# A decoder trunk whose weight blocks are stored as even columns then odd columns, and read in turn

## The chip, the cores and the metric

The kernel runs on one core of one Trainium2 chip. The metric is the device time of one execution in microseconds (us); lower is better. All the weights, some 410 MB, are read from device memory once in each execution. The weights are laid out by the host before the launch, and that is not timed.

## The reference, cut to what matters

Two layers on 256 tokens of width 2048. Each has a mixer (a recurrent block in the first, dilated attention in the second) and an MLP with a squared ReLU, each behind an RMSNorm, and the trunk ends with one more RMSNorm. Everything is float32.

```python
def _mlp(h, w1, w2):                                   # w1 2048 x 8192, w2 8192 x 2048
    u = jnp.einsum('bsd,df->bsf', h, w1)
    u = jnp.square(jax.nn.relu(u))
    return jnp.einsum('bsf,fd->bsd', u, w2)

def _rglru_block(h, w_in, conv_w, conv_b, w_a, b_a, w_x, b_x, lam, w_out):
    xg = jnp.einsum('bsd,de->bse', h, w_in)            # 2048 x 5120
    ...
    return jnp.einsum('bse,ed->bsd', y, w_out)         # 2560 x 2048

def _dilated_attention_block(h, w_qkv, w_o):
    qkv = jnp.einsum('bsd,de->bse', h, w_qkv).reshape(bsz, s, 3, N_HEADS, HEAD_DIM)
    ...
    return jnp.einsum('bse,ed->bsd', o.reshape(bsz, s, D_MODEL), w_o)

def reference(x, ...):
    for i in range(DEPTH):                             # DEPTH = 2
        h = _rmsnorm(x, mix_norm[i])
        ...
        x = x + _rglru_block(...) if i % 2 == 0 else x + _dilated_attention_block(...)
        x = x + _mlp(_rmsnorm(x, mlp_norm[i]), mlp_w1[i], mlp_w2[i])
    return _rmsnorm(x, final_norm)
```

## The kernel before

**Split operands.** A float32 operand is cut in two: a high part that the copy into the type float32r makes (ScalarE, line 132) and a low part, the difference (VectorE, line 136). A product of matrices is then three TensorE products: high by high, high by low, low by high. All of them are issued by one helper, `mm` (line 201), so that nearly every TensorE row of the profile has that line; the names of the tiles tell them apart. `whi` and `wlo` are the parts of a block of weights; `xT`, `aT` and `sT` are parts of tokens, 128 wide at a time.

**Weights.** They come in blocks of 128 partitions by 2048 float32 (1 MB, `UW`), one transfer each, into the tile `raw` (or `q...` in the MLP). A block holds four pieces of 512 columns in a row, one for each of four steps over the contracted dimension.

**Two kinds of products.** A matmul on TensorE has a stationary operand, 128 by 128, which is loaded first (LDWEIGHTS), and a moving operand that is streamed past it, up to 512 columns.

- In `stand_w` the weights are stationary and the tokens move, 256 columns at a time. The profile names such products `g<-xT,whi` or `acc<-xT,whi`: the first name behind the arrow is the moving operand. They serve w_in, the q and k part of w_qkv, and w1.
- In `stand_x` and in the `product` of the MLP's groups the tokens are stationary and the weights move, 512 columns at a time. The profile names them `acc<-whi,aT`, `tr<-whi,sT` and so on, with the weights first. They serve w_out, the v part of w_qkv, w_o and w2. Each step calls `three` (line 310) for its three products; where `border` is set the last one is cut into two of 256 columns. The last rows of the last chunk have their own loop, `last_half`, in pieces of 256 columns.

**The second MLP matrix** is worked in groups of two by two blocks with seven products in place of eight; sums of weight blocks are made by VectorE (line 649) and by accumulating transfers from GpSimd's queue (line 645), sums of tokens by VectorE. These sums are made element by element on whole blocks.

**Order.** A list of items, one for each block of weights, is written out by the planners (`plan_rec`, `plan_mlp`, `plan_att`). Ahead of each item the loads of blocks five ahead and the splits of blocks two or three ahead are issued; behind it, what its result feeds. Nothing reorders the list, and each engine works it off in turn.

**Layouts.** `_layout` permutes the weights on the host. `move` gives the blocks of w_out, w_v and w_o, and a line of its own gives w2: (block, partition, step, column), the 512 columns of a piece one behind another.

The stages in the order of the profile: recurrent input products to about 250 us, w_out to 370, first MLP to 1010, v, q, k and attention to 1345, w_o to 1430, second MLP to the end.

## Time and profile before

| what | value |
|---|---|
| median of 3 executions | 2086.66 us (2085.65 to 2086.71) |
| span of the profiled execution, first to last instruction | 2083.2 us |
| median less span: what lies around the instructions | 3.5 us |
| TensorE matmuls busy | 2071.8 us (99%) |
| VectorE / ScalarE / GpSimd busy | 82% / 61% / 4% |
| read from device memory | 409.58 MB, 198 GB/s over the span |
| mean granted TensorE clock | 0.999 |

The profile gives no other time for the profiled execution than its span, so 2083.2 + 3.5 us stands for it. A matmul's own duration (277 ns for 256 columns, 390 ns for 512) holds the time from its first column to its last result; matmuls overlap, so the pace is read from the spacing of their starts or from the length of a long unbroken piece of one kind, not from the mean duration. The column "busy" counts overlapping time once.

### The profile page before, as it was taken

The page shows a single profiled execution, that of the slowest core. Times are in us where ns is not written, and L with a number is a line of the kernel's source. Part 1 is how long each engine was busy: PE and PEld are TensorE (multiplying, and loading weights), DVE is VectorE, ACT ScalarE, POOL GpSimd, SP SyncE. Part 2 cuts the span into 40 slices and gives each one's busy share as a digit, 9 for nine tenths or more (in the row PEclk, how much of TensorE's full clock was granted, in tenths as well). Part 3 has the DMA queues.
Part 4 walks back from the last instruction along what each step waited for, and adds up shares of the span by engine and source line. Part 5 has one row for each costly group of instructions (what it writes and reads, how often), then busy time and mean ns, then how long its engine had stood idle before and what let it go on. Part 6 is the DMA issues. An engine that isn't in the chain of part 4 may idle for free.

```text
span 2083.2 us, 33880 instructions
## 1 busy us (share of the span) xinstructions
PE 2071.8 (99%) x14231; PEld 1905.6 (91%) x14231; DVE 1713.7 (82%) x1927; ACT 1278.7 (61%) x1388; POOL 86.7 (4%) x83
## 2 busy tenths in 40 slices
PE   9999999999999999999999999999999999999998
PEld 8999988999999999899889999889999998998996
DVE  7988855799999989998558868756999999899985
ACT  7777865566566656665546556555666566566553
POOL 0111100000000000000000000000000000000001
PEclk9999999999999999999999999999999999999999
DMA  8555555677887788777554455456778877887773
GB/s 300 204 204 193 200 202 182 236 230 243 298 245 255 251 261 268 222 259 228 204 182 173 171 182 180 171 183 235 242 243 285 248 258 244 266 276 218 251 240 141
DMA packets 68920, 472.59 MB, mean 227 GB/s; under 512 B 7584, under 2 KB 7712, under 8 KB 13472
## 3 DMA queue, kind: packets, MB, share of 16 engines
q1 hardware_dynamic: 60560, 411.45, 53.4%
q0 software_dynamic: 8064, 58.72, 14.4%
q8 instruction: 111, 1.82, 0.3%
q14 instruction: 41, 0.34, 0.0%
q10 hardware_dynamic: 144, 0.26, 0.0%
HBM read 409.58 MB, written 2.10 MB: 198 GB/s over the span
## 4 chain that ended last, share of the span: by engine, by line
PE 98%; DMA 1%; DVE 0%; ACT 0%; SPq 0%; issue 0%; ACTq 0%
PE acc L201 46%; PE g L201 32%; PE tr L201 19%; PE tr L242 1%; DMA raw<-in_w_in 0%; DMA xg<-in_xT 0%; PE tr L816 0%; DVE wlo L136 0%; ACT whi L132 0%; ACT xT L1039 0%; SPq L1025 0%; ACT junk L904 0%; PE tr L276 0%; SPq L1023 0%; DVE xc L902 0%
## 5 line engine op out<-in xcount | busy, mean ns | idle before, releaser
L132 ACT ACTIVATE whi<-raw 128x2048 fp32r<-128x2048 f32 (+1 forms) x309 | 569.7, 1846 | 403.8 <-PE acc L201 195.9
L136 DVE TENSOR_TENSOR wlo<-raw,whi 128x2048 fp32r<-128x2048 f32 (+1 forms) x309 | 678.0, 2197 | 108.0 <-ACT whi L132 107.5
L201 PE MATMUL g<-xT,whi 128*128 128x256 f32 x3649 | 626.6, 277 | 0.0
L201 PEld LDWEIGHTS g<-xT,whi 128*128 128x128 f32 x3649 | 550.0, 188 | 0.0
L201 PE MATMUL g<-xT,wlo 128*128 128x256 f32 x1824 | 503.9, 276 | 0.1
L201 PE MATMUL acc<-xT,whi 128*128 128x256 f32 x2724 | 466.5, 277 | 0.4 <-ACT whi L132 0.3
L201 PEld LDWEIGHTS acc<-xT,whi 128*128 128x128 f32 x2724 | 410.8, 188 | 1.7 <-ACT whi L132 1.2
L201 PE MATMUL acc<-xT,wlo 128*128 128x256 f32 x1360 | 376.0, 276 | 0.0
L201 PEld LDWEIGHTS g<-xT,wlo 128*128 128x128 f32 x1824 | 342.6, 188 | 0.2 <-DVE wlo L136 0.2
L201 PE MATMUL acc<-whi,aT 128*128 128x512 f32 (+1 forms) x1064 | 334.1, 389 | 0.0
L132 ACT ACTIVATE whi<-q 128x2048 fp32r<-128x2048 f32 x112 | 215.1, 1921 | 130.0 <-PE g L201 94.6
L136 DVE TENSOR_TENSOR wlo<-q,whi 128x2048 fp32r<-128x2048 f32 x112 | 256.1, 2286 | 30.6 <-ACT whi L132 30.6
L201 PEld LDWEIGHTS acc<-xT,wlo 128*128 128x128 f32 x1360 | 255.4, 188 | 0.5 <-DVE wlo L136 0.4
L201 PEld LDWEIGHTS acc<-whi,aT 128*128 128x128 f32 x1064 | 199.3, 188 | 40.2
L201 PE MATMUL tr<-whi,sT 128*128 128x512 f32 (+1 forms) x728 | 221.0, 376 | 0.0
L201 PE MATMUL acc<-wlo,aT 128*128 128x512 f32 (+1 forms) x532 | 206.4, 388 | 0.0
L132 ACT ACTIVATE whi<-qT 128x2048 fp32r<-128x2048 f32 x56 | 107.6, 1921 | 125.6 <-PE g L201 92.8
L201 PEld LDWEIGHTS tr<-whi,sT 128*128 128x128 f32 x728 | 136.6, 188 | 34.1 <-issue 7.0
L201 PE MATMUL tr<-whi,aT 128*128 128x512 f32 (+1 forms) x462 | 145.2, 383 | 0.0
L136 DVE TENSOR_TENSOR wlo<-qT,whi 128x2048 fp32r<-128x2048 f32 x56 | 128.1, 2287 | 11.9 <-ACT whi L132 11.9
L201 PE MATMUL tr<-wlo,sT 128*128 128x512 f32 x336 | 131.0, 390 | 0.0
L201 PEld LDWEIGHTS acc<-wlo,aT 128*128 128x128 f32 x532 | 100.0, 188 | 19.7
(169 smaller groups left out, 2127.1 us busy)
## 6 DMA issues: line engine op xcount, KB each, us to landing
raw<-in_w SPq DMA_DIRECT2D x172, 1024.0 KB, 6.3
q<-in_w SPq DMA_DIRECT2D x84, 1024.0 KB, 7.2
raw<-in_w_in SPq DMA_DIRECT2D x35, 1024.0 KB, 4.9
raw<-in_w_qk SPq DMA_DIRECT2D x32, 1024.0 KB, 4.8
q<-q POOLq DMA_DIRECT2D x28, 1024.0 KB, 12.5
q<-qT POOLq DMA_DIRECT2D x28, 1024.0 KB, 7.0
raw<-in_w_out SPq DMA_DIRECT2D x20, 1024.0 KB, 4.8
raw<-in_w_v SPq DMA_DIRECT2D x16, 1024.0 KB, 4.8
```

The lines of the kernel that those rows point to most:

```text
L132: nc.scalar.activation(split[i][0][:, s], r, AF.Copy)
L136: nc.vector.tensor_sub(split[i][1][:, s], r, split[i][0][:, s].bitcast(F32))
L201: nc.tensor.matmul(o, l, r, start=start, stop=stop, skip_group_check=True)
L242: nc.tensor.transpose(tr[:, k, t * 128:(t + 1) * 128], xc[n][:, t, c:c + 128], ident)
```

## The change

The columns of every 512-column piece of the moving weights (w_out, w_v, w_o, w2) are stored in another order: the 256 even columns first, then the 256 odd ones. The products that move these weights read them through a view with two dimensions, 256 steps outside and 2 inside: element 0 of the first half, element 0 of the second half, element 1 of the first half, and so on. In a partition's memory two columns that follow each other in the stream lie 256 elements (1024 bytes) apart, and the next step goes back by 255 elements. The columns reach the array in their old order, so the output, its layout and every later step stay as they were. Where a product covers 256 of the 512 columns, it reads 128 of each half.

No instruction is added, removed or moved on any engine or queue, and no tile or transfer has another size: the list of instructions is the same but for the line numbers and the access pattern of the moving operand. Blocks in `stand_w`, the gate weights and the token tiles stay as they were.

```diff
     def three(bank, xh, xl, hi, lo, opens, closes, border):
 
-        mm(bank, xh, hi, opens, False)
-        mm(bank, xh, lo, False, False)
+        mm(bank, xh, in_turn(hi), opens, False)
+        mm(bank, xh, in_turn(lo), False, False)
         cut = 256 if border else 512
         for at in range(0, 512, cut):
-            mm(bank[:, at:at + cut], xl, hi[:, at:at + cut], False, closes and at + cut == 512)
+            mm(bank[:, at:at + cut], xl, in_turn(hi, at, cut), False, closes and at + cut == 512)
+
+    def in_turn(w, at=0, n=512):
+
+        return w.rearrange("p (t q) -> p q t", t=2)[:, at // 2:(at + n) // 2, :]
...
             for s in halves:
                 for j, k in enumerate(rows[1]):
                     xh, xl = aT(k)[:, 128:256], aT(k)[:, 384:512]
-                    w = slice(j * 512 + s.start, j * 512 + s.stop)
-                    mm(acc[1][:, s], xh, hi[:, w], False, False)
-                    mm(acc[1][:, s], xh, lo[:, w], False, False)
-                    mm(acc[1][:, s], xl, hi[:, w], False, j == 3)
+                    wh, wl = (in_turn(w[:, j * 512:(j + 1) * 512], s.start, 256) for w in (hi, lo))
+                    mm(acc[1][:, s], xh, wh, False, False)
+                    mm(acc[1][:, s], xh, wl, False, False)
+                    mm(acc[1][:, s], xl, wh, False, j == 3)
...
     def move(w):
         k, n = w.shape
-        return c(w.reshape(k // 512, 4, 128, n // 512, 512).transpose(3, 0, 2, 1, 4)).reshape(-1, 128, UW)
+        w = w.reshape(k // 512, 4, 128, n // 512, 256, 2).transpose(3, 0, 2, 1, 5, 4)
+        return c(w).reshape(-1, 128, UW)
...
-        w2 = mlp_w2[i].reshape(4, 4, 4, 128, 4, 512).transpose(0, 4, 1, 3, 2, 5)
+        w2 = mlp_w2[i].reshape(4, 4, 4, 128, 4, 256, 2).transpose(0, 4, 1, 3, 2, 6, 5)
```

## Prediction

> **What bounds the kernel now.** I read the page first: its span, the busy shares, and the chain that ended last.

> ```profile
> span 2083.2 us, 33880 instructions
> PE 2071.8 (99%) x14231; PEld 1905.6 (91%) x14231; DVE 1713.7 (82%) x1927; ACT 1278.7 (61%) x1388; POOL 86.7 (4%) x83
> PE 98%; DMA 1%; DVE 0%; ACT 0%; SPq 0%; issue 0%; ACTq 0%
> ```

> TensorE is busy 99% of the span and makes 98% of the chain. Outside its work there are only 2083.2 - 2071.8 = 11.4 us, at the two ends. So whatever makes TensorE's stream longer makes the kernel longer by the same amount, and whatever makes it shorter counts until another engine becomes the bound. The next question is its pace, which busy time cannot tell since matmuls overlap. The chain in order of time has long pieces of one kind, and their length over their count is the spacing.

> ```profile
> 55.10 21.78 PE acc L201 x192
> 252.07 16.34 PE acc L201 x72
> ```

> The first piece (start, length, count) is 192 products of 256 moving columns in the recurrent stage: 21.78 / 192 = 0.1134 us each. The second is 72 products of 512 moving columns in w_out, the kind that the change touches: 16.34 / 72 = 0.2269 us. The second is twice the first, so there is nothing per instruction to see; both come to **0.443 ns per column**. The stream is paced by columns.

> **What the change touches.** It adds, removes and moves no instruction. The transfers and the splits keep their sizes and their contiguous patterns, and the sums of blocks work element by element, so the new order in a block is nothing to them: they cost what they cost, and if one of these took longer, TensorE's work would cover it as it does now. The one thing that is new is the order of addresses in the moving operand. How many products that is stands in the groups of TensorE by line and shape:

> ```profile
> L201 PE MATMUL acc<-whi,aT 128*128 128x512 f32 x1048 | 331.3, 390 | 0.0
> L201 PE MATMUL acc<-wlo,aT 128*128 128x512 f32 x524 | 204.1, 390 | 0.0
> L201 PE MATMUL tr<-whi,sT 128*128 128x512 f32 x616 | 198.9, 393 | 0.0
> L201 PE MATMUL tr<-whi,aT 128*128 128x512 f32 x434 | 139.6, 390 | 0.0
> L201 PE MATMUL tr<-wlo,sT 128*128 128x512 f32 x336 | 131.0, 390 | 0.0
> L201 PE MATMUL tr<-wlo,aT 128*128 128x512 f32 x224 | 87.4, 390 | 0.0
> L201 PE MATMUL acc<-whi,xT 128*128 128x512 f32 x254 | 79.8, 392 | 0.0
> L201 PE MATMUL acc<-whi,sT 128*128 128x512 f32 x212 | 68.9, 389 | 0.0
> L201 PE MATMUL acc<-wlo,xT 128*128 128x512 f32 x128 | 50.1, 391 | 0.0
> L201 PE MATMUL acc<-wlo,sT 128*128 128x512 f32 x112 | 43.6, 389 | 0.0
> ...
> L201 PE MATMUL tr<-whi,sT 128*128 128x256 f32 x112 | 22.2, 280 | 0.0
> ...
> L201 PE MATMUL tr<-whi,aT 128*128 128x256 f32 x28 | 5.5, 280 | 0.0
> ...
> L201 PE MATMUL acc<-whi,sT 128*128 128x256 f32 x24 | 4.8, 280 | 0.0
> ...
> L201 PE MATMUL acc<-whi,aT 128*128 128x256 f32 x16 | 3.0, 282 | 0.0
> L201 PE MATMUL acc<-wlo,aT 128*128 128x256 f32 x8 | 2.3, 283 | 0.0
> ...
> L201 PE MATMUL acc<-whi,xT 128*128 128x256 f32 x4 | 0.8, 280 | 0.0
> ```

> The ten rows of 512 columns add up to 3888, the six of 256 to 192, which is 96 more in units of 512: **3984 products of 512 columns**, 2.040 million columns. No record is missing: `whi` products are twice the `wlo` products in every pair (1048 + 8 to 524 + 4, 616 + 56 to 336, 434 + 14 to 224, 254 + 2 to 128, 212 + 12 to 112). At 0.2269 us they take 904 us now, 43% of the span, and each 0.01 ns per column is worth 20.4 us. The other products move tokens (`xT` ahead of the weight's name) and are not touched.

> **What a column costs when its neighbour is 1024 bytes away.** No row of this trace has it: every large stream here is read contiguously. It must be bounded.

> From below: a gain is possible, since the pace need not be the array's own. The trace has one slower stream to hold it against, ten bfloat16 products at the start.

> ```profile
> 1.25 4.45 PE L201 MATMUL g<-junk 128*128 128x512 bf16 x10 [1.25 <-DVE junk L1005]
> L201 PE MATMUL g<-junk 128*128 128x512 bf16 x10 | 4.4, 631 | 1.3 <-DVE junk L1005 1.3
> ```

> Ten products in 4.45 us, the last of which takes 0.63: nine spacings of 0.424 us. If that is the array at half its pace, which I suppose and the trace does not show, full pace is 0.212 us for 512 columns, an estimate, and the float32r stream at 0.2269 loses 7% to something, about one column time in 16. That loss grows with columns, so it belongs to reading them or to their type. This is the lower end: 0.0147 us less for each of 3984 products, -59 us.

> [...]

> From above: what does it cost an engine to fetch a float32 column by itself? The nearest rows are ScalarE and VectorE on the same weights, in two sizes.

> ```profile
> L132 ACT ACTIVATE whi<-raw 128x2048 fp32r<-128x2048 f32 x291 | 558.4, 1919 | 402.1 <-PE acc L201 195.9 <-PE g L201 84.9 <-PE tr L201 41.7
> L132 ACT ACTIVATE whi<-raw 128x512 fp32r<-128x512 f32 x16 | 9.3, 620 | 1.7 <-DMA raw<-in_w_first 1.7
> L136 DVE TENSOR_TENSOR wlo<-raw,whi 128x2048 fp32r<-128x2048 f32 x291 | 665.2, 2286 | 106.4 <-ACT whi L132 106.1
> L136 DVE TENSOR_TENSOR wlo<-raw,whi 128x512 fp32r<-128x512 f32 x16 | 10.5, 688 | 1.6 <-ACT whi L132 1.4
> ```

> ScalarE takes (1919 - 620) / 1536 = 0.846 ns for one more column, VectorE (2286 - 688) / 1536 = 1.040 ns. TensorE streams the same data at 0.443 ns, twice as fast as ScalarE. That is why I expect a loss: an engine that gets two columns in the time in which ScalarE gets one probably fetches neighbours together, and after the change no two columns that follow each other are neighbours. If each then needs a fetch of its own, the pace falls to that of one column at a time. I take ScalarE's **0.846 ns** for it. Exactly half of today's pace, 2 x 0.443 = 0.886, and the pace of the ten products, 0.424 / 512 = 0.829, lie on both sides of it; VectorE's 1.040 is the upper end.

> [...]

> **The sum.** (0.846 - 0.443) ns x 2.040 million columns = +822 us. Nothing hides it: TensorE has no idle time inside these stages. Then 2083.2 + 822 + 3.5 us of what lies around the span (median 2086.66 less 2083.2) gives **2908 us**. With 0.829 it is 2874, with 0.886 it is 2990, with 1.040 it is 3304. The other engines only wait longer.

> **Rivals.**

> *The pace stays.* If the addresses are made one by one and the memory answers each at full pace, the order is free and the time is 2087 us. For it: spacing is exactly proportional to columns in two kinds of streams from two kinds of tiles, as if the array set it. Against it: the 7% against the bfloat16 stream. [...]

> *The lost sixteenth goes.* If the 7% is a wait in reading one run of addresses (a place in memory that needs a pause before it answers again), two runs in turn give each place twice the time, and the wait is gone. Price: up to -59 us, 2028 us. It decides as soon as the pause is shorter than one column's time in the other half. VectorE would not stop it; in the first MLP it stands so:

> ```profile
> 410.00:1010.00 600.00, 600.00 (x4030) 548.31 (x4030) 541.48 (x511) 365.85 (x311) 24.20 (x28) 1.00 0.78 250
> ```

> Of 600 us TensorE has all and VectorE 541.5 (the columns are the stretch, then busy time of matmuls, weight loads, VectorE, ScalarE and GpSimd). The stretch holds less than a third of the 59 us to be gained, some 20 us, and VectorE's slack in it is 58.5 us. Against this rival: it needs a memory that likes jumps better than runs, and nothing here shows one.

> [...]

> *A small loss*, a pause at some steps only, lies anywhere between 2091 and 2870 us; I have no row for it.

> **How the numbers follow.** Forecast, one column at a time (2874 to 2990): 0.33. The pace of VectorE or worse: 0.11. A small loss: 0.09. Pace stays: 0.20. The sixteenth goes, wholly or in part: 0.27. So faster by over 0.2% (4 us, about what a measurement of this kernel can tell from no change) 0.27, within 0.2% 0.20, slower 0.53. The range must reach over both signs: from the lower end, 2028, to VectorE's pace, 3304. Only about a tenth lies outside, above it. The forecast's own range is 2874 to 2990.

> **What would show it.** In the changed profile the long piece of 72 products at the start of w_out should take 72 x 0.433 = 31.2 us in place of 16.34, and that of 192 at 55.10 should stay at 21.78; TensorE's share stays at 99% and VectorE's falls to some 59%. [...] If the piece of 192 changed too, or VectorE's rows grew, the cause would lie outside the moving reads and my reasoning would be wrong.

## The result, and the profile after

| | before | changed |
|---|---|---|
| median | 2086.26 us | 2052.54 us |
| all executions | 2085.65 to 2086.71 | 2049.91 to 2054.89 |
| ratio (95% interval) | | 0.9839 (0.9825 to 0.9853) |

The kernel before has one execution more here than in the table ahead of the change. One execution of a later kernel (w2 alone), in a slower state at 7365 us, is left out of all medians and ratios. The changed kernel is 1.6% faster, where I had forecast it 39% slower. The page of the changed kernel answers to the three lines that opened the prediction (span; busy time; the chain that ended last):

```profile
span 2049.2 us, 33880 instructions
PE 2031.2 (99%) x14231; PEld 1910.6 (93%) x14231; DVE 1712.1 (84%) x1927; ACT 1278.3 (62%) x1388; POOL 87.1 (4%) x83
PE 88%; DVE 5%; issue 3%; ACT 2%; DMA 1%; SPq 0%; ACTq 0%; DVEq 0%
```

TensorE's busy time fell by 40.6 us and the span by 34.0. TensorE made 98% of the chain before and makes 88% now: other engines have come into it, VectorE first. The pieces of the chain that the prediction named say what happened to the pace (start, length, count):

```profile
78.92 21.91 PE acc L201 x192
...
103.65 21.78 PE acc L201 x192
...
251.29 15.54 PE acc L201 x72
```

Products that move tokens stayed at 21.78 us for 192 (one piece has 0.13 us more). The 72 products that move w_out went from 16.34 to 15.54 us: **0.2158 us each in place of 0.2269**. The stream runs at 0.4215 ns per column, not at 0.846.

Over 3984 products that is 3984 x 0.0111 = 44 us. The median fell by 33.7. Most of the other 10 us is a wait, of which the list of TensorE's waits shows a part (in total, times, longest):

```profile
PE tr L201 <- DVE xc L657: 4.6, 14, 0.3
PE g L201 <- DVE junk L1009: 1.3, 1, 1.3
```

The list of the kernel before has no row like the first. But the list counts only time in which TensorE is idle, and a product's last results overlap a short wait: each lasts 0.38 us in the rows below, at a spacing of 0.216. By the starts of the products there are 28 such places: in 14 of them (the row's) the first product behind the wait starts 0.49 us later than the pace gives, in 14 others 0.23 us later, 10.1 us in all; in the kernel before the same places lose 1.2 us. The products right behind them lose 1.1 us more than before. One of the places of the second kind in order of time, TensorE and then VectorE, in the first MLP (start, length):

```profile
528.59 0.38 PE L201 MATMUL tr<-wlo,aT 128*128 128x512 f32 x1
528.80 0.38 PE L201 MATMUL tr<-whi,aT 128*128 128x512 f32 x1
529.25 0.45 PE L201 MATMUL tr<-whi,sT 128*128 128x512 f32 x1
```

```profile
525.88 2.29 DVE L136 TENSOR_TENSOR wlo<-qT,whi 128x2048 fp32r<-128x2048 f32 x1
528.09 0.42 DVE L572 TENSOR_TENSOR aT<-uu,aT 128x256 fp32r<-128x256 f32 x1
528.42 0.68 DVE L657 TENSOR_TENSOR xc<-xc,tr 128x512 f32<-128x512 f32 x1
```

The next group product needs a `tr` bank that VectorE is still emptying into `xc`. That take ends at 528.42 + 0.68 = 529.10, the product starts at 529.25, and the gap to the product before it is 0.45 us in place of 0.216. VectorE had no pause ahead of it: its three rows follow each other. In the kernel before the same place stood so:

```profile
537.12 0.39 PE L201 MATMUL tr<-whi,aT 128*128 128x512 f32 x1
537.35 0.43 PE L201 MATMUL tr<-whi,sT 128*128 128x512 f32 x1
536.48 0.68 DVE L653 TENSOR_TENSOR xc<-xc,tr 128x512 f32<-128x512 f32 x1
```

There the product kept its spacing of 0.23 us and started 0.19 us behind the end of the take (537.16); now it starts 0.15 us behind it. So this take had only some 0.04 us to spare before the change. The first question is why two places in turn are read faster than one run, and the second is whether VectorE's queue is what gives a quarter of the gain back.

### The profile page after: what moved, and what is told of

Read it like the earlier page. It is cut to its first block, busy times and chain, and to the rows that moved or that the text cites. A ratio compares the mean times of both kernels' runs of the same rounds, so it can differ in the third digit from the quotient of the medians.

```text
span 2049.2 us, 33880 instructions
## 1 busy us (share of the span) xinstructions
PE 2031.2 (99%) x14231; PEld 1910.6 (93%) x14231; DVE 1712.1 (84%) x1927; ACT 1278.3 (62%) x1388; POOL 87.1 (4%) x83
## 4 chain that ended last, share of the span: by engine, by line
PE 88%; DVE 5%; issue 3%; ACT 2%; DMA 1%; SPq 0%; ACTq 0%; DVEq 0%
PE acc L201 44%; PE g L201 31%; PE tr L201 13%; DVE wlo L136 2%; ACT whi L132 2%; DVE xc L657 1%; DVE qT L653 1%; DMA q<-in_w 0%; DVE aT L572 0%; PE tr L242 0%; DMA xg<-in_xT 0%; PE tr L820 0%; DVE uu L563 0%; ACT xg L244 0%; DVE xT L218 0%
## 5 line engine op out<-in xcount | busy, mean ns | idle before, releaser
L132 ACT ACTIVATE whi<-raw 128x2048 fp32r<-128x2048 f32 (+1 forms) x309 | 569.0, 1844 | 375.7 <-PE acc L201 201.8
L136 DVE TENSOR_TENSOR wlo<-raw,whi 128x2048 fp32r<-128x2048 f32 (+1 forms) x309 | 677.0, 2196 | 96.4 <-ACT whi L132 95.4
L201 PE MATMUL g<-xT,whi 128*128 128x256 f32 x3649 | 627.7, 277 | 0.0
L201 PEld LDWEIGHTS g<-xT,whi 128*128 128x128 f32 x3649 | 550.5, 188 | 0.0
L201 PE MATMUL g<-xT,wlo 128*128 128x256 f32 x1824 | 504.5, 277 | 0.0
L201 PE MATMUL acc<-xT,whi 128*128 128x256 f32 x2724 | 466.6, 277 | 0.2 <-ACT whi L132 0.2
L201 PEld LDWEIGHTS acc<-xT,whi 128*128 128x128 f32 x2724 | 410.9, 188 | 1.3 <-ACT whi L132 1.1
L201 PE MATMUL acc<-xT,wlo 128*128 128x256 f32 x1360 | 376.3, 277 | 0.4 <-DVE wlo L136 0.4
L201 PEld LDWEIGHTS g<-xT,wlo 128*128 128x128 f32 x1824 | 342.5, 188 | 0.4 <-DVE wlo L136 0.4
L201 PE MATMUL acc<-whi,aT 128*128 128x512 f32 (+1 forms) x1064 | 322.6, 378 | 0.0
L132 ACT ACTIVATE whi<-q 128x2048 fp32r<-128x2048 f32 x112 | 214.7, 1917 | 117.8 <-PE g L201 91.9
L136 DVE TENSOR_TENSOR wlo<-q,whi 128x2048 fp32r<-128x2048 f32 x112 | 256.1, 2287 | 26.9 <-ACT whi L132 26.4
L201 PEld LDWEIGHTS acc<-xT,wlo 128*128 128x128 f32 x1360 | 255.3, 188 | 0.9 <-DVE wlo L136 0.8
L201 PEld LDWEIGHTS acc<-whi,aT 128*128 128x128 f32 x1064 | 200.6, 189 | 27.4
L201 PE MATMUL tr<-whi,sT 128*128 128x512 f32 (+1 forms) x728 | 213.7, 366 | 5.5 <-DVE xc L657 4.6
L201 PE MATMUL acc<-wlo,aT 128*128 128x512 f32 (+1 forms) x532 | 200.8, 377 | 0.0
L132 ACT ACTIVATE whi<-qT 128x2048 fp32r<-128x2048 f32 x56 | 107.5, 1920 | 126.5 <-PE g L201 91.5
L201 PEld LDWEIGHTS tr<-whi,sT 128*128 128x128 f32 x728 | 137.4, 189 | 33.9 <-issue 16.0
L201 PE MATMUL tr<-whi,aT 128*128 128x512 f32 (+1 forms) x462 | 140.1, 373 | 0.0
L136 DVE TENSOR_TENSOR wlo<-qT,whi 128x2048 fp32r<-128x2048 f32 x56 | 128.1, 2287 | 7.2 <-ACT whi L132 5.6
L201 PE MATMUL tr<-wlo,sT 128*128 128x512 f32 x336 | 127.4, 379 | 0.0
L201 PEld LDWEIGHTS acc<-wlo,aT 128*128 128x128 f32 x532 | 100.6, 189 | 13.4
```

The lines of the kernel that those rows point to most:

```text
L132: nc.scalar.activation(split[i][0][:, s], r, AF.Copy)
L136: nc.vector.tensor_sub(split[i][1][:, s], r, split[i][0][:, s].bitcast(F32))
L201: nc.tensor.matmul(o, l, r, start=start, stop=stop, skip_group_check=True)
```

## The experiments

### The order by itself

A kernel of products alone: one stationary tile for each type, and for each order 40 products in a row, of 512 columns unless the row says less. In the code, `two(t, q)` cuts `t * q` columns into `t` runs of `q` and reads one column of each run in turn; in the other patterns, the order of the letters behind the arrow is the order of reading.

```diff
+    ("again", lambda w: w[:, 0:512]),
+    ("halves", two(2, 256)), ("quarter", two(4, 128)), ("sixteen", two(16, 32)), ("evenodd", two(256, 2)),
+    ("swapd", lambda w: w[:, 0:512].rearrange("p (b t q) -> p b q t", t=2, q=4)),
+    ("swapb", ... q=2), ("swaph", ... q=8), ("swapp", ... q=16), ("swapz", ... q=64),
+    ("runsb", lambda w: w[:, 0:512].rearrange("p (t q r) -> p q t r", t=2, r=2)), ("runsd", ... r=4),
+    ("stepb", lambda w: w[:, 0:1024].rearrange("p (q t) -> p q t", t=2)[:, :, 0]),
...
```

> A kernel of products alone, 40 in a row of each kind, all of 512 columns unless said, to measure the spacing by the order in which the moving operand is read; the trunk's computation is left out. Known from the changed kernel: columns one behind another 227 ns, two halves in turn 216 ns. Theory 'place': neighbours in memory read one behind another conflict in a small unit of memory; then every order whose next column lies in another unit gives 216 (quarters, sixteen parts, apart by 4 to 64 columns), while pairs swapped within four columns and runs of 16 or 64 columns keep 227. Theory 'form': a plain pattern of step 1 is read in a wide way that loses a sixteenth, any pattern whose innermost step is not 1 is read column by column at 216; then also pairs 2 columns apart, even columns before odd ones, and every second column of 1024 give 216, and any innermost run (2, 4, 16, 64 columns) gives 227. Theory 'distance': two far places are needed; then only halves, quarters and 64 apart give 216, and 2 to 16 apart give 227. The bfloat16 series: 216 in both orders if the loss belongs to the four-byte type. 256 token columns: 113 plain and 108 to 110 in turn. Output written in pairs of two places: 227 if the array's output does not mind, more if it does.

TensorE in order of time. A row is one series; the start of the next row less its own, over 40, is the spacing.

```profile
19.44 8.79 PE L73 MATMUL bank<-halves,st 128*128 128x512 f32 x40
28.07 9.25 PE L73 MATMUL bank<-again,st 128*128 128x512 f32 x40
37.16 11.46 PE L73 MATMUL bank<-quarter,st 128*128 128x512 f32 x40
48.45 17.57 PE L73 MATMUL bank<-sixteen,st 128*128 128x512 f32 x40
65.83 18.24 PE L73 MATMUL bank<-evenodd,st 128*128 128x512 f32 x40
83.89 8.82 PE L73 MATMUL bank<-swapd,st 128*128 128x512 f32 x40
92.54 9.24 PE L73 MATMUL bank<-swapb,st 128*128 128x512 f32 x40
101.62 8.80 PE L73 MATMUL bank<-swaph,st 128*128 128x512 f32 x40
110.26 8.80 PE L73 MATMUL bank<-swapp,st 128*128 128x512 f32 x40
118.89 8.80 PE L73 MATMUL bank<-swapz,st 128*128 128x512 f32 x40
127.52 13.76 PE L73 MATMUL bank<-runsb,st 128*128 128x512 f32 x40
141.11 10.18 PE L73 MATMUL bank<-runsd,st 128*128 128x512 f32 x40
151.12 9.77 PE L73 MATMUL bank<-runsp,st 128*128 128x512 f32 x40
...
169.84 18.29 PE L73 MATMUL bank<-stepb,st 128*128 128x512 f32 x40
187.95 9.64 PE L73 MATMUL bank<-offa,st 128*128 128x512 f32 x40
197.44 9.49 PE L73 MATMUL bank<-offh,st 128*128 128x512 f32 x40
...
224.61 8.81 PE L73 MATMUL bank<-bplain,sbf 128*128 128x512 bf16 x39
233.25 19.54 PE L73 MATMUL bank<-bhalves,sbf 128*128 128x512 bf16 x40
252.17 5.40 PE L73 MATMUL bank<-tall,st 128*128 128x256 f32 x40
```

| order of 512 float32 columns | ns for one product |
|---|---|
| one run (`again`) | 227 |
| two halves in turn; two places 4, 8, 16 or 64 columns apart | 216 |
| two places 2 columns apart (`swapb`) | 227 |
| four quarters; sixteen parts in turn | 282; 434 |
| even then odd columns; every second of 1024 | 452; 453 |
| two halves in turn, 2 or 4 columns at a time | 340; 250 |

So the loss that I had put at one sixteenth (227 against 216 ns) is in reading, and it goes with two places in turn; the plain bfloat16 series has 216 as well. My price is there too: sixteen places cost 434 ns, 0.849 ns per column, where I had taken 0.846. But all my theories are off somewhere. "Distance" falls with 4 columns apart at 216. "Form" falls with `swapb`, whose innermost step is not 1 either and which keeps 227. "Place" had quarters and sixteen parts at 216. And bfloat16 halves in turn, which I expected at 216, take 473 ns by this reading (the next series is of another type; the next kernel has 484). Output written in pairs of two places (`opairs`) leaves a plain run at 227.

### More orders

```diff
+    ("fournear", lambda w: w[:, 0:512].rearrange("p (b t q) -> p b q t", t=4, q=4)), ("eightnear", ... t=8, q=4),
+    ("bythree", lambda w: w[:, 0:510].rearrange("p (b t q) -> p b q t", t=2, q=3)),
+    ("stepd", lambda w: w[:, 0:1024].rearrange("p (q t) -> p q t", t=4)[:, :, 0]),
+    ("twice", lambda w: w[:, 0:256, None].to_broadcast([128, 256, 2])),
...
```

> Products alone again (the trunk is left out), 40 in a row of each kind, to see what the order needs. Theory 'two places stay open': the reader of the moving operand can go on at two places of four columns (16 bytes) each without loss, and more places than two cost up to 0.85 ns per column. Then: halves 216; four places near one another (4 columns apart) 283 as the four quarters had, eight near ones between 283 and 435; every fourth column of 1024 (256 columns, each in a place of its own) 217, every third (256 columns) 160 to 217; two places 3 columns apart between 216 and 340; halves shifted by one column 216 to 240; halves 260 columns apart 216; each column twice 216. Tokens (256 columns): 113 plain, 112 in turn in one or in two blocks of 128. Rival 'only far places': near ones cost more than far ones at the same number. For bfloat16, whose halves in turn took 484: if the unit is 4 bytes, pairs of columns in turn give 216; if it is the number of places, pairs and fours fall below 484 but stay above 216, and places 8 columns apart cost as much as halves.

```profile
27.00 10.91 PE L64 MATMUL bank<-fournear,st 128*128 128x512 f32 x40
37.74 19.36 PE L64 MATMUL bank<-eightnear,st 128*128 128x512 f32 x40
56.92 10.94 PE L64 MATMUL bank<-bythree,st 128*128 128x510 f32 x40
67.69 9.50 PE L64 MATMUL bank<-stepd,st 128*128 128x256 f32 x40
77.00 9.26 PE L64 MATMUL bank<-stepc,st 128*128 128x256 f32 x40
...
121.81 8.80 PE L64 MATMUL bank<-twice,st 128*128 128x512 f32 x40
130.44 4.95 PE L64 MATMUL bank<-tall,st 128*128 128x256 f32 x40
...
152.81 19.54 PE L64 MATMUL bank<-bhalves,sbf 128*128 128x512 bf16 x40
172.19 19.58 PE L64 MATMUL bank<-bnear,sbf 128*128 128x512 bf16 x40
191.61 11.01 PE L64 MATMUL bank<-bpairs,sbf 128*128 128x512 bf16 x40
```

In the same reading (start to next start, over 40) four near places cost 268 ns and eight 480, so nearness does not help and more than two places lose. Two places 3 columns apart, which do not fill a place of four, cost 269. Every fourth column (256 of them) costs 233, where 217 was expected. Each column read twice costs 216. In bfloat16 halves cost 484, places 8 columns apart as much, pairs of columns in turn 271 and fours 222 (`bquads`): there too the distance makes no difference, while the number of columns taken from a place at a time does. The eight near ones lie above the 435 that I had set as the end, and "two places stay open" cannot explain why every second column of a plain run costs 453: it leaves a place after two columns, and plain runs of whole places do not lose that.

### Two lanes

Several of the rows fit another picture, which I call two lanes. A place is taken to be four columns (16 bytes) from a multiple of four on, since two places 2 columns apart took 227 ns (`swapb`) and 4 apart 216 (`swapd`). In this picture the reader takes the stream two columns at a time, one lane for the even and one for the odd positions in the stream, and what counts is how many columns of a place **one lane** uses in a row. In a plain run a lane uses 2 of 4 (227 ns); in two halves in turn each lane has a run of its own and uses all 4 (216); with every second column, or sixteen places, it uses 1 (453, 434).

```diff
+    ("halvesb", lambda w: w[:, 0:1024].rearrange("p (t q s) -> p q t s", t=2, s=2)[:, :, :, 0]),
+    ("halvesd", ... s=4),
+    for n, names in ((256, ("tall", "tturn")), (128, ("short", "shortturn")), (192, ("mid", "midturn")),
+                     (320, ("long", "longturn"))):
...
```

> Products alone, 40 in a row of each kind (the trunk is left out). Theory 'two lanes', formed from the first two series: the reader takes the stream two columns at a time, one lane for the even and one for the odd places in the stream, and each lane needs about 1.77 ns for a new place of four columns (16 bytes) if it used it twice, and 0.88 ns per column if it used it once; it loses nothing if it uses a place four times. Rival 'places in all': what counts is how many columns of a 16-byte place the whole stream uses before it leaves. The series that tells them apart: every second column of two halves in turn (two of four columns used in a place, both by the same lane): two lanes 227 ns, places in all 452 as every second column of a plain run. Every second column plain: 452 by both. Every fourth column of two halves (256 columns): 226 by both. Pairs swapped 2 columns apart 227. Shorter products, with their weight load each: if a load of 128 columns is a floor of some 112 ns, 128 and 192 columns take 112 in both orders, 256 take 113 plain and 112 in turn, and 320 take 142 plain and 136 in turn; if there is no such floor, 128 take 57 and 54, 192 take 85 and 81.

```profile
28.13 9.25 PE L59 MATMUL bank<-halvesb,st 128*128 128x512 f32 x40
37.22 18.29 PE L59 MATMUL bank<-stepb,st 128*128 128x512 f32 x40
55.33 9.38 PE L59 MATMUL bank<-halvesd,st 128*128 128x256 f32 x40
64.53 9.51 PE L59 MATMUL bank<-stepd,st 128*128 128x256 f32 x40
...
87.76 4.63 PE L59 MATMUL bank<-tturn,st 128*128 128x256 f32 x40
92.23 4.58 PE L59 MATMUL bank<-short,st 128*128 128x128 f32 x40
...
110.07 6.05 PE L59 MATMUL bank<-long,st 128*128 128x320 f32 x40
115.96 5.60 PE L59 MATMUL bank<-longturn,st 128*128 128x320 f32 x40
121.62 8.58 PE L59 MATMUL bank<-bplain,sbf 128*128 128x512 bf16 x39
```

`halvesb` and `stepb` use two of four columns in every place; by the picture both go through the same lane in the first, and one through each in the second. They cost 227 and 453 ns, as two lanes foretold and "places in all" did not. The last rows show a floor as well: 128 columns take 111 ns, as long as 256 in turn (112), while 320 take 147 plain (142 were expected) and 136 in turn (5.60 less the last one's own 0.30, over 39). 192 columns take 113 plain and 112 in turn; no series here came in under 110 ns a product. One expectation failed: 256 columns in a plain run (`tall`) take 120 ns in these series, where 113 were expected and the kernel has 113; why is open.

### The order in the kernel, 4 columns apart

```diff
-        return w.rearrange("p (t q) -> p q t", t=2)[:, at // 2:(at + n) // 2, :]
+        return w[:, at:at + n].rearrange("p (b t q) -> p b q t", t=2, q=4)
```

> The changed kernel with the columns stored and read in turn 4 apart within every 8 in place of 256 apart within 512. Theory 'two lanes': the distance does not matter from 4 columns on, 2052 us as the changed kernel. Rival 'two far places of memory': back to 2086 us or above.

2056.30 us, ratio 0.9859 (0.9842 to 0.9877). The host stores the weights to match. The interval overlaps that of the changed kernel: 4 columns serve as well as 256 in the main. Its median lies 4 us above, and the 72 products at the start of w_out take 15.54 us in both. In its profile (2058.38 us, the longest of its four executions) the difference stands in products that this edit does not touch: many pieces of 144 products that move tokens in the MLP take 16.96 us, where the changed kernel has 16.34. Over all of these products that is 7 us; the two profiled spans differ by 6.1. Why they are slower is open.

### Sixteen parts in the kernel

```diff
-        return w.rearrange("p (t q) -> p q t", t=2)[:, at // 2:(at + n) // 2, :]
+        return w.rearrange("p (t q) -> p q t", t=16)[:, at // 16:(at + n) // 16, :]
```

> The changed kernel with sixteen parts of 32 columns read in turn in place of two halves; the weights are stored to match. Theory 'two places stay open': each column is a place of its own, 435 ns for 512 columns as in the series of products alone, so 3984 x (435 - 226.7) ns = 830 us more than before: 2916 us, near the 2908 of the prediction. Rival 'what a product costs alone is not what it costs in the kernel' (weight loads and other engines share the reading): over 2950 or under 2880 us.

The host stores the weights to match here too. 2909.3 us in one execution. The chain's piece at the start of w_out:

```profile
span 2907.2 us, 33880 instructions
...
252.59 31.32 PE acc L201 x72
```

The prediction had 31.2 us for this piece and 2908 us for the whole. Its forecast describes this kernel; the change is not this kernel.

### Where the gain is given back

Two kernels with half the change each. In the first w2 lies and is read as before; in the second w2 alone has the new order. The edit of the first is shown; the second asks for `not in`, and the host's layout follows in both.

```diff
     def in_turn(w, at=0, n=512):
+        if scope[0] in ("mlp", "end"):
+            return w[:, at:at + n]
```

> Only w_out, w_v and w_o lie in the new order and are read in turn; w2 and its products are as before. The changed kernel's trace has these stages shorter by 5.1, 3.1, 3.8 and 2.8 us, 14.8 in all, nearly the whole of 1248 products x 11 ns = 13.7 us. Theory 'VectorE in the MLP gives back': 2071.5 us, all of the gain of these stages. Rival 'stages lean on each other' (a stage that is faster makes the next one wait for its loads): clearly less gain than 14 us, 2075 us or more.

> Only w2 lies in the new order; w_out, w_v and w_o as before. 2736 products x 11 ns = 30 us gross. Theory 'VectorE in the MLP gives back': the two MLP stages gain 9.2 + 6.8 and the end 2.3, so about 2068 us, 11 us short of gross. Rival 'stages lean on each other': about 2058 us, the gross gain.

Without w2: 2072.52 us against 2085.63, ratio 0.9935 (0.9921 to 0.9950). That is -13.1 us of the 13.7 that 1248 products are worth at 11 ns. With w2 alone: 2064.84 us (median of three), ratio 0.9902 (0.9885 to 0.9918), -20.8 of 30 us; that lies between the 2068 of the theory and the 2058 of the rival, nearer the theory. The two gains add up to 33.9, the whole change has 33.7. So what is missing is missing in the products of w2; the stages do not take it from each other. TensorE's wait on `xc` is in the second kernel (its total is again 4.6 us in 14 times) and not in the first.

Then VectorE's queue, by the changed kernel with one edit more:

```diff
     def u_low(t, uu):
-        nc.vector.tensor_sub(t[:, 256:512], uu, t[:, 0:256].bitcast(F32))
+        nc.gpsimd.tensor_sub(t[:, 256:512], uu, t[:, 0:256].bitcast(F32))
```

> The changed kernel with one more edit: the low part of the MLP's squares (128 differences of 256 columns, 0.42 us each on VectorE) is made by GpSimd. Theory 'VectorE frees the banks late': its queue has 54 us less, the takes of the banks come earlier, and the waits ahead of the products on the tr banks (28 of 0.2 to 0.4 us, some 9 us in all) go or shrink: 2043 to 2047 us. Rival 'the wait is not VectorE's load but a fixed chain (transfer or split)': no gain, 2052 us; and if GpSimd's differences take over 2 us each, the products that read them wait, and it is slower.

2046.16 us, ratio 0.9808 (0.9792 to 0.9824): 6.4 us less than the changed kernel's median. GpSimd needs 2.03 us for what VectorE did in 0.42, yet the kernel is faster. TensorE's wait on that bank:

```profile
PE tr L201 <- DVE xc L657: 3.5, 4, 1.4
```

Four waits instead of fourteen, but longer ones: 3.5 us. By the starts of the products, the late ones behind a take lose 6.0 us in place of 10.1. So VectorE's queue gave back most of the 10 us, some 6; what gives back the rest was not taken apart.

### The tokens too

```diff
-                    nc.tensor.transpose(tr[:, k, ...], xc[n][:, t, c:c + 128], ident)
+                    nc.tensor.transpose(tr[:, k, ...], xc[n][:, t, c:c + 128], ident if gname == "mix1" else turn)
...
-            mm(ps, hi[:, s], x[:, 256:512], False, False)
+            mm(ps, hi[:, s], tokens(x[:, 256:512]), False, False)
...
+    def tokens(x):
+        if scope[0] == "att":
+            return x
+        return x.rearrange("p (b t q) -> p b q t", t=2, q=64)
```

> The changed kernel with the same order for the tokens as moving operand, but in the attention stage: the 128 tokens of a block are stored as even then odd ones (the host's copy of x; the identity that transposes is read in that order), and the products that move tokens read the two halves of each block in turn. About 8000 products of 256 columns, 113.3 to about 109 or 111.7 ns each: 13 to 34 us gross. Theory 'the order is worth the same for any moving operand': 2020 to 2040 us, less what VectorE gives back in the MLP stages (its share there is 90 to 93% by now), so about 2035. Rival 'VectorE takes it all': no more than 5 us below the changed kernel, 2048 to 2053 us.

> The kernel with tokens in turn, and the low part of the MLP's squares made by GpSimd as in the run with that edit alone. If VectorE is what gives the gain back in the MLP stages, this is 8 us or more below the kernel with tokens in turn, about 2025 us; if not, as in that run, 6 us below, or equal.

Tokens in turn: 2034.93 us, ratio 0.9754 (0.9739 to 0.9768). With the squares' low part on GpSimd as well: **2029.70 us, ratio 0.9726 (0.9710 to 0.9742)**, the fastest of all. A piece of 192 products of tokens in that last kernel:

```profile
102.98 21.44 PE acc L201 x192
```

21.44 / 192 = 0.1117 us in place of 0.1134. That is the floor of some 112 ns that short products showed, so about 8000 products gain 1.7 ns each, some 14 us. The medians of the changed kernel and of the kernel with tokens in turn lie 17.6 us apart; where the other 4 us come from is not shown. The GpSimd edit gains 5.2 us here, not the 8 that I expected if VectorE were all of it.

## Why the prediction was wrong

- **What bounds the kernel**: right. TensorE's pace set the time, and the change of pace came through nearly one to one (13.1 us of 13.7 without w2) until another engine was late.
- **What is touched, and how much**: right. 3984 products, and only their moving reads; token products kept 0.1134 us, no other instruction changed.
- **The lower end**: right in kind, a little far. The ten bfloat16 products at the start took 0.424 us each, and a series of them later in a kernel takes 216 ns each, about half, as I had supposed. Why the first ten are slow is not shown: the profile before has the granted clock at 1.00 there too (0.5 to 5.5 us). But half of 0.424 gave 212, and the fastest pace that a run shows is 215.8: 44 us gross, not 59.
- **The step that failed**: "If each then needs a fetch of its own, the pace falls to that of one column at a time." No two neighbours in the stream are neighbours in memory any more, that is true; but the reader does not need them to be: this order costs 0.4215 ns per column, where I had 0.846. In the picture of two lanes, which the runs bear out only in part, each lane has a run of its own and uses four columns of a place instead of two. I gave the price to an order that does not pay it. Orders that do pay are near it: sixteen places cost 0.849 ns, and the kernel that reads so takes 2909 us against 2908 (my terms add up to 2908.7). That the match is so close is luck: nothing here ties ScalarE's pace to TensorE's reading, and even columns before odd ones cost 0.88 ns, eight near places 0.94.
- **The rival that came true**: the lost sixteenth goes, at 0.27. The piece of 72 products, 15.3 us at the pace of 0.212 that it rests on, came at 15.54. The mechanism that I gave it is not borne out: if a place in memory needed a pause, four quarters and sixteen parts in turn would take 216 ns too, and they take 282 and 434. My reason against it, that it needs a memory that likes jumps better than runs, was a picture of memory and no row. The proportion of 227 and 113 ns to the columns was in rows, and the 7% against bfloat16 was my estimate from a row; both pointed at the reading of a plain run. A new order could go either way, and I should have weighed it so. The proportion held less than I read from it, though: 113 ns lies just above the floor of 112 that short products showed, so there was something per instruction right beneath the pace.
- **VectorE "would not stop it"**: half right. I compared averages, 541.5 of 600 us. VectorE has slack over the stage, but hardly any ahead of 28 takes of a `tr` bank, and there some 10 us of the 44 went. The trace before had it: the take shown above had 0.04 us to spare. The stretch, not the stage, decides.

## What to carry to other kernels

Measure the spacing of products in a long piece, and hold it against another type's spacing. Here the stream that was a few per cent slow, in proportion to its columns, was slow in reading, and its order in memory was worth a try. For float32 operands that the host lays out, two runs read in turn, four columns or more apart, took 216 ns where one run took 227; four or more runs in turn, or a step of two, took 268 to 480, and bfloat16 went from 216 to 484 with two halves in turn. This kernel, bound by one engine at 99%, gained only until the worst stretch of the next queue, so look for the waits that have almost no slack before counting the whole gain.
